# Decode tokens and the last inverse merge as whole 128 by 128 products, up weights in the main buffers, first results unpaused

## The chip, the cores and the metric

The kernel runs on one core of one Trainium2 chip. The metric is device time in microseconds. Three runs of the kernel before took 1026.06, 1026.82 and 1027.05 us; the median is 1026.82 us.

## What is computed

One decoder layer for 1024 prompt tokens and 64 decode tokens (8 sequences of 8 tokens). RMS-normalised input goes through one wide projection. A gated linear attention (GLA, 4 heads) and a gated DeltaNet (4 heads, keys and values 128 wide) run beside each other; each is gated, projected to 1024 channels, merged by sigmoid gates, projected again and added to the input; a per-layer embedding is added and a last RMSNorm follows. The part that the change is about most is the DeltaNet's chunk:

```python
    k_beta = k * beta[..., None]
    v_beta = v * beta[..., None]
    a_mat = jnp.where(strict, jnp.einsum('bhnid,bhnjd->bhnij', k_beta, k) * gamma, 0.0)
    t_mat = a_mat + jnp.eye(c, dtype=jnp.float32)
    solve = functools.partial(lax.linalg.triangular_solve, left_side=True, lower=True,
                              unit_diagonal=True)
    u = solve(t_mat, v_beta)
    w = solve(t_mat, k_beta * jnp.exp(decay)[..., None])
    qk = jnp.einsum('bhnid,bhnjd->bhnij', q, k) * gamma
    ...
    def step(s, inp):
        w_c, u_c, q_c, qk_c, k_c, d_c = inp
        v_new = u_c - jnp.einsum('bhcd,bhdv->bhcv', w_c, s)
        o_c = jnp.einsum('bhcd,bhdv->bhcv', q_c, s) + jnp.einsum('bhcs,bhsv->bhcv', qk_c, v_new)
        s = s * d_c[..., None, None] + jnp.einsum('bhcd,bhcv->bhdv', k_c, v_new)
        return s, o_c
```

The prompt starts from a zero state, the decode tokens from given states (`state_gla`, `state_gdn`, `state_conv`). All inputs and outputs are fp32.

## The kernel before

All activations lie with channels on the 128 partitions and tokens along the columns: 1024 prompt columns, then 64 decode columns. Every large product is made three times from split operands (`xh`, `xl` and `wh`, `wl`, type fp32r), in `prod`, one output tile of up to 416 columns after the other. These are called main products here. In the middle of the run they are those of the input projection (`ing`, `inza`, `inzb`, `ingsg`, `ingsh`), then come the up projections `py`, the output projection `ho` and the embedding `eg`, `ep`.

The branches are written as Python generators, run by `_Side`. After each six main products, `prod` calls `sd.tick()`, and each task goes one step on; `yield n` in a task lets n ticks pass. So TensorE's queue holds main products with a branch's small products strewn in between, in an order that is fixed when the program is built. Small products are plain fp32: the profiler shows two records for each (x2), and one for a transposing product.

The steps that the change touches:

- `conv_rest` (L781): short convolution of q, k or v of one head; the 64 decode columns go to `Ds`, a 128x64 tile. For q and k it makes token-row copies of the chunks (`ss`) and takes their squares; the decode columns get a product of their own (`ssS`, L840 for q, L842 for k).
- `gdn` (L852): decay matrix `Gm`, products `kq` (L898, L899; chunk 8 is that of the decode tokens), inverses of 32x32 blocks on VectorE (`B`), then merges to 64 (`z32`, `x32`) and to 128 (`z64` L974, `x64` L982, on 64x64 tiles of the array), then the chunk loop `ch` (L1006 to L1017), then rows out (`obT`, `obS` L1055).
- `gdn_sample` (L1062): the decode tokens against the given states: `sa` (L1081, then L1087 and L1091 on 64x64 tiles), and `dSb` (L1105), which updates the states in two products of 32 rows each.
- `gla` (L569): its decode part makes `attS` in two products of 64x64 (L718).
- `w_load`, `w_split`: a weight block is loaded to `wr`, then split by ScalarE (L173) and VectorE (L174). Most blocks go to `wh`, `wl` with three buffers each. The up weights go to `uh`, `ul`, in a pool `lp` that is opened when the pools of the branches are closed:

```python
    rec.close()
    lp = ctx.enter_context(tc.tile_pool(name="lp", bufs=1))
```

- `final` and `normed` (L1417, L1426): the last RMSNorm of column chunks 0 and 1 runs as a side task during the embedding of chunk 2; five ticks pass after each sum (`ssy`, L1422) and three before each store. Chunk 2 itself is done in two halves at the end of `embed` (L1463 to L1484).

Of the kernel before, what the change touches and what calls it, by code (L numbers as in the profile page):

```python
# [27 lines left out]
UW, HW = 1116, 512  # L28
# [3 lines left out]
C_ID, C_TRI, C_TRB, C_SEG, C_NEG, C_NGS, C_SCN, C_SEL, C_SL4 = 0, 128, 256, 384, 512, 640, 704, 768, 776  # L32
C_N = 780
# [70 lines left out]
def tile_hybrid_step(ctx: ExitStack, tc: tile.TileContext, xT, pT, wmain, wv0, wv1, wup, wout, wpg, wpl, wgate,  # L104
# [22 lines left out]
    def small(name):  # L127
        return kp.tile([P, P], F32, tag="sm", name=name, bufs=8)

    def col(name, w=NS):  # L130
        return kp.tile([P, NS], F32, tag="col", name=name, bufs=12)[:, 0:w]
# [19 lines left out]
    def bfree(n=1):  # L151
        sd.free_banks += n
# [199 lines left out]
    K = kp.tile([P, C_N], F32, tag="K", name="K")  # L352
    ident = K[:, C_ID:C_ID + P]
    tri = K[:, C_TRI:C_TRI + P]
    load(K, cst)

# [132 lines left out]
    def gdn_scalars():  # L489
# [32 lines left out]
        mm(ps[:, 32:36], K[:, C_TRB:C_TRB + P], gd[:, 8], start=True, stop=True)  # L522
        mm(ps[:, 64:96], ones, gd[:, 0:8], start=True, stop=True)
        mm(ps[:, 96:100], K[:, C_SEG:C_SEG + P], gd[:, 8], start=True, stop=True)
# [42 lines left out]
    def gla(hp):  # L567
# [131 lines left out]
        att_s, kem = small(f"attS{hp}"), small(f"kem{hp}")  # L699
        G.memset(att_s, 0.0)  # L700
        G.memset(kem, 0.0)
# [9 lines left out]
        for h2 in range(2):  # L711
            r = slice(64 * h2, 64 * h2 + 64)
            V.tensor_copy(kem[r, r], keS[r])
        yield from sd.banks(1)
        ps = rps(f"attS{hp}")
        for h2 in range(2):
            r = slice(64 * h2, 64 * h2 + 64)
            mm(ps[r, 0:NS], kS[r], qS[r], start=True, stop=True)  # L718
            V.copy_predicated(att_s[r, r], mks[r], ps[r, 0:NS])
        PE.transpose(ps[:, 128:256], kem, ident)  # L720
# [38 lines left out]
    cb, sss, sks, resv = {}, {}, {}, {}  # L759
# [21 lines left out]
    def conv_rest(kind, h, R, S):  # L781
# [12 lines left out]
        Ds = col(f"Ds{kind}{h}")  # L794
# [5 lines left out]
        if kind == 2:  # L800
# [15 lines left out]
            cb[kind, h] = (R, Ds)  # L816
# [6 lines left out]
        ss, r = sss[h], slice(64 * i, 64 * i + 64)  # L823
# [23 lines left out]
        cb[kind, h] = (D, Ds, R)  # L847

    def gdn(h):
# [20 lines left out]
        while (0, h) not in cb or (1, h) not in cb:  # L870
            yield 0
        q, q_s, _ = cb[0, h]
        k, k_s, kt = cb[1, h]
# [15 lines left out]

        for g in range(5):  # L890
            yield from sd.banks(1)
            ps = rps(f"kq{h}{g}")
            for c in range(2 * g, min(2 * g + 2, 9)):
                s = slice(c * P, (c + 1) * P) if c < 8 else slice(NP, T)
                m = P if c < 8 else NS
                o = (c % 2) * 256
                kc, qc = (k[:, s], q[:, s]) if c < 8 else (k_s, q_s)
                mm(ps[0:m, o:o + m], kc, kc, start=True, stop=True)  # L898
                mm(ps[0:m, o + P:o + P + m], kc, qc, start=True, stop=True)  # L899
                V.scalar_tensor_tensor(AT[0:m, s], ps[0:m, o:o + m], nbr2[0:m, c:c + 1], Gm[0:m, s],  # L900
                                       op0=ALU.mult, op1=ALU.mult)
                V.scalar_tensor_tensor(Gm[0:m, s], ps[0:m, o + P:o + P + m], rk[0:m, c:c + 1], Gm[0:m, s],
                                       op0=ALU.mult, op1=ALU.mult)
# [7 lines left out]
        for j in range(2):  # L911
            r = slice(32 * j, 32 * j + 32)
            load(scr_a[h][32 + j].rearrange("(s t) -> s t", s=32), AT[r, NP + 32 * j:NP + 32 * j + 32])
# [671 lines left out]
```

## Time and profile before

| | |
|---|---|
| median of three runs | 1026.82 us |
| the profiled execution | 1021.09 us |
| its span (first to last instruction) | 1019.3 us |
| granted TensorE clock, mean | 0.996 |
| TensorE busy | 1003.2 us, 7042 records |
| VectorE busy | 620.0 us, 1400 instructions |
| ScalarE busy | 397.1 us, 956 instructions |
| GpSimd busy | 36.6 us, 53 instructions |

The page's second part shows TensorE at 90% or more in 39 of 40 slices. A record's duration includes the fill of the array, and records overlap; what a product costs is the distance from its start to the start of the next one. A main product of 384 columns starts 0.17 us after the one before it while its record says 0.34 us.

### The profile page before, as it was taken

The page shows a single profiled execution, that of the slowest core. Times are in us where ns is not written, and L with a number is a line of the kernel's source. Part 1 is how long each engine was busy: PE and PEld are TensorE (multiplying, and loading weights), DVE is VectorE, ACT ScalarE, POOL GpSimd, SP SyncE. Part 2 cuts the span into 40 slices and gives each one's busy share as a digit, 9 for nine tenths or more (in the row PEclk, how much of TensorE's full clock was granted, in tenths as well). Part 3 has the DMA queues.
Part 4 walks back from the last instruction along what each step waited for, and adds up shares of the span by engine and source line. Part 5 has one row for each costly group of instructions (what it writes and reads, how often), then busy time and mean ns, then how long its engine had stood idle before and what let it go on. Part 6 is the DMA issues. An engine that isn't in the chain of part 4 may idle for free.

```text
span 1019.3 us, 17637 instructions
## 1 busy us (share of the span) xinstructions
PE 1003.2 (98%) x7042; PEld 962.0 (94%) x7042; DVE 620.0 (61%) x1400; ACT 397.1 (39%) x956; POOL 36.6 (4%) x53
## 2 busy tenths in 40 slices
PE   9999999999999999999999999999999999999996
PEld 7999999979999999999999999999999999999996
DVE  6785743455776679667866775554488323653347
ACT  6764634334314523452354224331233111533335
POOL 0000001011100001000000000000000000000000
PEclk9999999999999999999999999999999999999998
DMA  9011112222133021322132222003456332221015
GB/s 320 2 42 63 50 52 78 87 73 74 51 109 95 22 75 45 92 68 63 59 96 73 62 95 70 12 24 112 134 158 173 111 129 107 63 83 42 21 48 190
DMA packets 67027, 84.73 MB, mean 83 GB/s; under 512 B 26797, under 2 KB 51313, under 8 KB 66945
## 3 DMA queue, kind: packets, MB, share of 16 engines
q1 hardware_dynamic: 66672, 83.22, 26.1%
q8 instruction: 55, 0.90, 0.4%
q10 hardware_dynamic: 272, 0.39, 0.1%
q14 instruction: 28, 0.22, 0.1%
HBM read 65.38 MB, written 18.21 MB: 82 GB/s over the span
## 4 chain that ended last, share of the span: by engine, by line
PE 91%; DVE 5%; DMA 1%; ACT 1%; issue 1%; POOL 0%; SPq 0%; DVEq 0%; ACTq 0%
PE ing L288 12%; PE ingsg L288 9%; PE py L288 9%; PE ho L288 9%; PE ingsh L288 8%; PE eg L288 8%; PE inzb L288 5%; PE inza L288 5%; PE ep L288 2%; PE inka L288 2%; PE inqa L288 2%; PE v L402 2%; PE v L403 2%; PE v L405 1%; DVE B L927 1%; DVE tm L925 1%
## 5 line engine op out<-in xcount | busy, mean ns | idle before, releaser
L173 ACT CAST wh<-wr 128x1024 fp32r<-128x1024 f32 x59 | 61.8, 1049 | 164.3 <-PE ho L288 41.0
L174 DVE TENSOR_TENSOR wl<-wr,wh 128x1024 fp32r<-128x1024 f32 x59 | 72.0, 1222 | 72.0 <-ACT wh L173 71.1
L288 PE MATMUL ing<-xh,wh 128*128 128x384 f32 (+1 forms) x288 | 97.8, 340 | 0.0
L288 PE MATMUL ing<-xl,wh 128*128 128x384 f32 (+1 forms) x288 | 94.7, 329 | 0.0
L288 PE MATMUL ing<-xh,wl 128*128 128x384 f32 (+1 forms) x288 | 94.2, 327 | 0.0
L288 PE MATMUL ingsh<-xh,wh 128*128 128x384 f32 (+1 forms) x192 | 66.6, 347 | 0.0
L288 PE MATMUL ingsg<-xh,wh 128*128 128x384 f32 (+1 forms) x192 | 65.6, 342 | 0.0
L288 PE MATMUL eg<-Hh,wh 128*128 128x416 f32 (+1 forms) x192 | 63.6, 331 | 0.0
L288 PE MATMUL eg<-Hh,wl 128*128 128x416 f32 (+1 forms) x192 | 63.2, 329 | 0.0
L288 PE MATMUL ingsg<-xl,wh 128*128 128x384 f32 (+1 forms) x192 | 63.0, 328 | 0.0
L288 PE MATMUL ho<-Mh,wh 128*128 128x416 f32 (+1 forms) x192 | 63.0, 328 | 0.0
L288 PE MATMUL ingsh<-xl,wh 128*128 128x384 f32 (+1 forms) x192 | 62.9, 328 | 0.0
L288 PE MATMUL ingsg<-xh,wl 128*128 128x384 f32 (+1 forms) x192 | 62.9, 327 | 0.0
L288 PE MATMUL ingsh<-xh,wl 128*128 128x384 f32 (+1 forms) x192 | 62.9, 327 | 0.0
L288 PE MATMUL ho<-Ml,wh 128*128 128x416 f32 (+1 forms) x192 | 62.8, 327 | 0.0
L288 PE MATMUL ho<-Mh,wl 128*128 128x416 f32 (+1 forms) x192 | 62.8, 327 | 0.0
L288 PE MATMUL eg<-Hl,wh 128*128 128x416 f32 (+1 forms) x192 | 62.7, 327 | 0.0
L288 PEld LDWEIGHTS ing<-xh,wh 128*128 128x128 f32 x288 | 54.1, 188 | 2.2 <-issue 1.1
L288 PEld LDWEIGHTS ing<-xl,wh 128*128 128x128 f32 x288 | 54.2, 188 | 0.3 <-issue 0.2
L288 PEld LDWEIGHTS ing<-xh,wl 128*128 128x128 f32 x288 | 54.1, 188 | 0.2 <-issue 0.2
L789 DVE SCALAR_TENSOR_TENSOR D<-R,cw,D 128x1112 f32<-128x1112 f32 x36 | 49.2, 1368 | 2.6 <-ACT D L787 2.1
L1393 DVE SCALAR_TENSOR_TENSOR H<-ho,xres 128x416 f32<-128x416 f32 (+1 forms) x24 | 12.8, 535 | 57.7 <-PE ho L288 57.7
(432 smaller groups left out, 2764.1 us busy)
## 6 DMA issues: line engine op xcount, KB each, us to landing
wr<-in_wmain SPq DMA_DIRECT2D x38, 512.0 KB, 3.5
wr<-in_wpg SPq DMA_DIRECT2D x13, 512.0 KB, 3.5
xres<-in_xT SPq DMA_DIRECT2D x8, 544.0 KB, 4.5
wr<-in_wup SPq DMA_DIRECT2D x16, 256.0 KB, 2.7
wr<-in_wout SPq DMA_DIRECT2D x8, 512.0 KB, 3.6
gt<-gscrg SPq DMA_DIRECT2D x16, 208.0 KB, 2.3
gt<-gscrh SPq DMA_DIRECT2D x16, 208.0 KB, 2.4
out_yT<-y SPq DMA_DIRECT2D x8, 416.0 KB, 2.5
```

The costliest lines, as they stand in the source:

```text
L173: a = A.copy(wh, wr).ins
L174: b = (eng or V).tensor_tensor(wl, wr, wh.bitcast(F32), op=ALU.subtract).ins
L288: mm(ps[:, :w], l_, r_, start=i == 0, stop=i == len(seq) - 1)
L402: mm(ps[:, :n], h_, a_, start=k == 0, stop=False)
L403: mm(ps[:, :n], l_, a_, start=False, stop=False)
L405: mm(ps[:, :n], h_, b_, start=False, stop=k == 7)
L789: V.scalar_tensor_tensor(D[:, :n], R[:, i:n + i], cw[:, 4 * ci + i:4 * ci + i + 1], D[:, :n], op0=ALU.mult, op1=ALU.add)
L925: V.tensor_tensor(tv, Bv[:, j:j + 1, j + 1:32].broadcast_to([NBLK, j, n]), Bv[:, 0:j, j:j + 1].broadcast_to([NBLK, j, n]), op=ALU.mult)
L927: V.tensor_tensor(Bv[:, 0:j, j + 1:32], Bv[:, 0:j, j + 1:32], tv, op=ALU.add)
L1393: V.scalar_tensor_tensor(H[m][:, o:o + w], ps[:, :w], 0.5, xres[m][:, o:o + w], op0=ALU.mult, op1=ALU.add)
```

## The change

- The decode columns of q and k of one head share one 128x128 tile `kqs` (k in columns 0 to 63, q in 64 to 127); v has a tile `vs` with zeros behind it. One whole transposing product replaces L840 and L842, one whole product replaces chunk 8 of L898 and L899, and one transposing product replaces the two of L992.
- `Cs` (128x128, lower rows zero) holds the decode tokens' two 64x64 matrices side by side; L1087, L1091 and L1055 become whole 128x128 products.
- `z64` and `x64` run as whole products of 64 columns; GpSimd clears the rows of `X` and `Z` that would disturb them. `X` and `Z` get a ninth block (`HW` 576).
- The second pause of `gdn` before `z32` is 13 ticks and not 10.
- `dSb`'s first product is held behind the chunk loop's last product (`after`).
- `attS` is one whole product from a masked copy `km`.
- The up weights use `hw_main`.
- `final` waits one tick and not five, `normed` none and not three.
- The constants tile is split; `small` has 11 buffers, `col` 8.

```diff
-        yield from sd.banks(1)
-        ps = rps(f"ssS{h}{i}")
-        if kind == 0:
-            mm(ps[r, 0:P], Ds, ident, start=True, stop=True)
-        else:
-            PE.transpose(ps[r, 0:P], Ds, ident)
-        A.activation(ps[r, 0:P], ps[r, 0:P], AF.Square, accum_out=ss[r, 9 * i + 8:9 * i + 9])
-        bfree()
...
+        if (1 - kind, h) in cv:
+
+            yield from sd.banks(1)
+            ps = rps(f"ssS{h}")
+            PE.transpose(ps[:, 0:P], sm, ident)
...
+            if g == 4:
+                mm(ps[:, 0:P], kq_s, kq_s, start=True, stop=True)
...
-        yield 10
+        yield 13
...
+        G.memset(X[64:128, 0:8], 0.0)
+        G.memset(Z[0:64, 0:8], 0.0)
         for c in range(8):
-            mm(zv[64:128, c], ATv[0:64, c, 64:128], X[0:64, c], start=True, stop=True)
-        A.copy(Z[64:128], zv[64:128])
+            mm(zv[:, c], ATv[:, c], X[:, c], start=True, stop=True)
+        A.copy(Z[64:128, 0:8], zv[64:128])
...
         for c in range(8):
-            mm(zv[0:64, c], Z[64:128, c], ATv[64:128, c, 64:128], start=True, stop=True)
+            mm(zv[:, c], Z[:, c:c + 2].rearrange("p c n -> p (c n)"), ATv[:, c, 64:128], start=True, stop=True)
...
-            mm(ps[:, 0:P], Gm[:, s], vn, start=True, stop=True)
+            lastpe[h] = mm(ps[:, 0:P], Gm[:, s], vn, start=True, stop=True).ins
...
-        PE.transpose(ps[:, 0:NS], os_[hi], K[hi, C_ID + NS:C_ID + P])
-        A.mul(ob[h][:, NP:T], ps[:, 0:NS], nwh[:, 1:2])
+        PE.transpose(ps[:, 0:P], os_, ident)
+        A.mul(ob[h][:, NP:T], ps[:, NS:P], nwh[:, 1:2])
...
-        mm(ps[lo, 256:384], AT[lo, NP:T], vtS[lo], start=True, stop=True)
-        vn = small(f"vnS{h}")
-        A.mul(vn[lo], ps[lo, 256:384], brk[lo, 8:9])
+        mm(ps[:, 256:384], Cs, vtS, start=True, stop=True)
+        vn = vtS
+        A.mul(vn, ps[:, 256:384], brk[:, 8:9])
         yield 5
-        mm(ps[hi, 384:512], Gm[lo, NP:T], vn[lo], start=True, stop=True)
...
+        mm(ps[:, 384:512], Cs, vn, start=True, stop=True)
...
-            mm(pd[g], ktS[r], vb[r], start=True, stop=True)
+            e = mm(pd[g], ktS[r], vb[r], start=True, stop=True).ins
+            if g == 0 and h in lastpe:
+                after(e, lastpe[h])
...
-            wlist += [(wup[8 * br + m], 4, P, hw_up)]
+            wlist += [(wup[8 * br + m], 4, P, hw_main)]
...
-            yield 5
+            yield 1
         yield from normed(parts, pss, last)
 
-    def normed(parts, pss, last, waits=3, sizes=(2, 2, 2, 2)):
+    def normed(parts, pss, last, waits=0, sizes=(2, 2, 2, 2)):
```

TensorE's queue where the first head's states are updated. Before, as built:

```order
L288 MATMUL ing_2_4204<-xh_574,wl 128x320
L1105 MATMUL dSb_4256<-vbb_4166,ktS_3885 128x512
L1016 MATMUL ch_4211<-vn_4230,R_2518 128x128
L1017 MATMUL ch_4211<-vn_4230,Gm_2626 128x128
L1105 MATMUL dSb_4257<-vbb_4166,ktS_3885 128x512
L288 MATMUL ing_2_4204<-xh_574,wh 128x320
```

The same place in the changed kernel:

```order
L288 MATMUL ing_2_4215<-xh_580,wh 128x320
L1040 MATMUL ch_4222<-vn_4241,R_2527 128x128
L1041 MATMUL ch_4222<-vn_4241,Gm_2635 128x128
L1127 MATMUL dSb_4267<-vbb_4177,ktS_2866 128x512
L1127 MATMUL dSb_4268<-vbb_4177,ktS_2866 128x512
L288 MATMUL ing_2_4215<-xl_581,wh 128x320
```

The two `dSb` products stood apart, with two products of the chunk loop between them; now they stand side by side.

ScalarE's queue around the last two blocks of the z gate (`ztzb`), ahead of the up projection. Before:

```order
L1245 ACTIVATE ztzb_7300<-inzb_1_7275 128x384
L1245 ACTIVATE ztzb_7331<-inzb_2_7304 128x320
L1048 ACTIVATE ob_7311<-obT_7335,nwh 128x512
...
L1245 ACTIVATE ztzb_7406<-inzb_1_7381 128x384
L1245 ACTIVATE ztzb_7435<-inzb_2_7410 128x320
L173 CAST uh<-wr 128x512 x7
```

In the changed kernel:

```order
L1269 ACTIVATE ztzb_7308<-inzb_1_7270 128x384
L173 CAST wh<-wr 128x512
L1269 ACTIVATE ztzb_7337<-inzb_2_7312 128x320
...
L1269 ACTIVATE ztzb_7414<-inzb_1_7389 128x384
L173 CAST wh<-wr 128x512
L1269 ACTIVATE ztzb_7443<-inzb_2_7418 128x320
L173 CAST wh<-wr 128x512 x5
```

The first split of an up weight stood behind the last z block; now one stands a whole z block earlier and one more ahead of the last.

VectorE's queue at the end, from the embedding block before the last to the last chunk's squares (`y` are final results of chunk 1). Before:

```order
L1487 SCALAR_TENSOR_TENSOR et_10216<-et_10216,ep_10219 128x256
L1448 TENSOR_TENSOR y_10318<-H_8739,rsy_10138 128x416
L1488 SCALAR_TENSOR_TENSOR H_8739<-et_10216,H_8739 128x256
L1448 TENSOR_TENSOR y_10322<-H_8834,rsy_10138 128x416
L1448 TENSOR_TENSOR y_10322<-H_8925,rsy_10138 128x416
L1493 TENSOR_TENSOR acc_9248<-acc_9248,es_10217 128x256
L1448 TENSOR_TENSOR y_10326<-H_9016,rsy_10138 128x416
L1474 SCALAR_TENSOR_TENSOR et_10256<-et_10256,es_10257 128x128
L1446 SCALAR_TENSOR_TENSOR y_10326<-H_9107,pc,rsy_10138 128x416
L1477 TENSOR_TENSOR H_8834<-H_8834,et_10256 128x128
L1478 TENSOR_TENSOR es_10257<-H_8834 128x128
```

In the changed kernel:

```order
L1507 SCALAR_TENSOR_TENSOR et_10249<-et_10249,ep_10252 128x256
L1508 SCALAR_TENSOR_TENSOR H_8747<-et_10249,H_8747 128x256
L1513 TENSOR_TENSOR acc_9256<-acc_9256,es_10250 128x256
L1494 SCALAR_TENSOR_TENSOR et_10289<-et_10289,es_10290 128x128
L1497 TENSOR_TENSOR H_8842<-H_8842,et_10289 128x128
L1498 TENSOR_TENSOR es_10290<-H_8842 128x128
```

All `y` of chunks 0 and 1 now stand earlier, from the first embedding block of chunk 2 on.

## Rows read from the trace of the kernel before

**Rows 1.** The page's first part (engine, busy us and share of the span, instructions) and its fourth, the chain that ended last, by engine.

```profile
PE 1003.2 (98%) x7042; PEld 962.0 (94%) x7042; DVE 620.0 (61%) x1400; ACT 397.1 (39%) x956; POOL 36.6 (4%) x53
PE 91%; DVE 5%; DMA 1%; ACT 1%; issue 1%; POOL 0%; SPq 0%; DVEq 0%; ACTq 0%
```

**Rows 2.** Whom TensorE waited for, whole span: us in total, times, longest.

```profile
PE z L951 <- DVE X L943: 1.2, 1, 1.2
PE ssy L1471 <- DVE acc L1493: 1.1, 1, 1.1
PE o L562 <- DVE ssqa L553: 1.1, 1, 1.1
PE py L288 <- ACT uh L173: 1.0, 1, 1.0
```

**Rows 3.** Timeline of TensorE around `x64` of the first head (one main product left out): start us, duration us, what, rows x columns of the array's tile, partitions x columns that stream, count of records, and in brackets the idle time before.

```profile
335.35 0.34 PE L288 MATMUL ing<-xh,wl 128*128 128x384 f32 x1
335.62 1.14 PE L982 MATMUL x<-AT,Z 64*64 64x64 f32 x16
...
336.98 0.34 PE L288 MATMUL ing<-xl,wh 128*128 128x384 f32 x1
```

**Rows 4.** The same view where whole fp32 products with few columns follow each other (cumulated decays, `gds`).

```profile
124.07 0.30 PE L521 MATMUL gds<-gd,K 128*128 128x32 f32 x2
124.21 0.36 PE L522 MATMUL gds<-gd,K 128*128 128x4 f32 x2
124.43 0.39 PE L523 MATMUL gds<-gd,ones 128*128 128x32 f32 x2
```

**Rows 5.** The same view around a single whole fp32 product of 128 columns among main products (one main product left out).

```profile
377.40 0.33 PE L288 MATMUL ing<-xh,wh 128*128 128x384 f32 x1
377.57 0.38 PE L1012 MATMUL ch<-R,AT 128*128 128x128 f32 x2
...
377.97 0.34 PE L288 MATMUL ing<-xh,wl 128*128 128x384 f32 x1
```

**Rows 6.** The same view around `ssS`: of q (L840, a product on 64 columns of the array), and of k (L842, a transposing product); one main product is left out in each.

```profile
331.67 0.34 PE L288 MATMUL ing<-xh,wl 128*128 128x384 f32 x1
331.93 0.43 PE L840 MATMUL ssS<-K,Ds 128*64 128x128 f32 x2
...
332.58 0.33 PE L288 MATMUL ing<-xl,wh 128*128 128x384 f32 x1
...
346.25 0.34 PE L288 MATMUL inza<-xh,wl 128*128 128x384 f32 x1
346.42 0.27 PE L842 MATMUL ssS<-K,Ds 128*64 128x128 f32 x1
...
346.70 0.33 PE L288 MATMUL inza<-xl,wh 128*128 128x384 f32 x1
```

**Rows 7.** The same view around a 64x64 product of the decode tokens (`sa`, L1091), between a whole product and two main products, one of them left out.

```profile
384.80 0.39 PE L1007 MATMUL ch<-S,D 128*128 128x128 f32 x2
385.12 0.43 PE L1091 MATMUL sa<-vnS,Gm 64*64 64x128 f32 x2
...
385.76 0.34 PE L288 MATMUL ing<-xl,wh 128*128 128x384 f32 x1
```

**Rows 8.** The same view around the state updates `dSb`: of the first head (the two apart, two products of the chunk loop between them and a main product behind them left out), and of the last (side by side; the same three left out).

```profile
391.62 0.31 PE L288 MATMUL ing<-xh,wl 128*128 128x320 f32 x1
391.86 1.12 PE L1105 MATMUL dSb<-vbb,ktS 32*128 32x512 f32 x2
...
393.55 1.12 PE L1105 MATMUL dSb<-vbb,ktS 32*128 32x512 f32 x2
...
394.86 0.31 PE L288 MATMUL ing<-xl,wh 128*128 128x320 f32 x1
...
667.74 0.31 PE L288 MATMUL inzb<-xh,wl 128*128 128x320 f32 x1
...
668.42 1.13 PE L1105 MATMUL dSb<-vbb,ktS 32*128 32x512 f32 x4
...
669.76 0.34 PE L288 MATMUL inzb<-xl,wh 128*128 128x384 f32 x1
```

**Rows 9.** The same view around a decode row out, `obS` (one main product left out).

```profile
431.93 0.34 PE L288 MATMUL ing<-xh,wl 128*128 128x384 f32 x1
432.19 0.27 PE L1055 MATMUL obS<-K,os 64*128 64x64 f32 x1
...
432.65 0.31 PE L288 MATMUL ing<-xl,wh 128*128 128x320 f32 x1
```

**Rows 10.** Timeline of GpSimd, the one clearing of 512 columns in the first head's stretch.

```profile
330.48 0.53 POOL L1070 MEMSET kqm<- 128x512 f32 x1 [71.09 <-PE z L974]
```

**Rows 11.** Timelines of VectorE and of ScalarE at the end of the run.

```profile
1008.87 0.42 DVE L1493 TENSOR_TENSOR acc<-acc,es 128x256 f32<-128x256 f32 x1
1009.21 0.58 DVE L1448 TENSOR_TENSOR y<-H,rsy 128x416 f32<-128x416 f32 x1
1009.71 0.28 DVE L1474 SCALAR_TENSOR_TENSOR et<-et,es 128x128 f32<-128x128 f32 x1
1009.91 0.65 DVE L1446 SCALAR_TENSOR_TENSOR y<-H,pc,rsy 128x416 f32<-128x416 f32 x1
...
1009.42 1.28 ACT L1428 ACT_TABLE_LOAD   x1
```

More of the change, by code (lines that the diff above doesn't have):

```diff
@@ L351, in tile_hybrid_step @@
         load(wg[hp][0:16, :], wgate[:, hp * P:(hp + 1) * P])
-    K = kp.tile([P, C_N], F32, tag="K", name="K")
+    K = kp.tile([P, C_K], F32, tag="K", name="K")
     ident = K[:, C_ID:C_ID + P]
-    tri = K[:, C_TRI:C_TRI + P]
-    load(K, cst)
+    load(K, cst[:, 0:C_K])
+    tri, trb, seg = (small(n) for n in ("tri", "trb", "seg"))
+    for t, o in ((tri, C_TRI), (trb, C_TRB), (seg, C_SEG)):
+        load(t, cst[:, o:o + P])
     mk = kp.tile([P, P], U8, tag="mk", name="mk")
@@ L697, in gla @@
         load(gla_p[hp], Sprev[:, 1024 - P:1024])
-        att_s, kem = small(f"attS{hp}"), small(f"kem{hp}")
-        G.memset(att_s, 0.0)
-        G.memset(kem, 0.0)
+        att_s, kem, km = small(f"attS{hp}"), small(f"kem{hp}"), small(f"km{hp}")
+        for t in (att_s, kem, km):
+            G.memset(t, 0.0)
         S0 = [half(f"S0a{hp}{g}")[:, :512] for g in range(2)]
@@ L713, in gla @@
             V.tensor_copy(kem[r, r], keS[r])
+            V.tensor_copy(km[r, r], kS[r])
         yield from sd.banks(1)
         ps = rps(f"attS{hp}")
+        mm(ps[:, 0:NS], km, qS, start=True, stop=True)
+        PE.transpose(ps[:, 128:256], kem, ident)
         for h2 in range(2):
             r = slice(64 * h2, 64 * h2 + 64)
-            mm(ps[r, 0:NS], kS[r], qS[r], start=True, stop=True)
             V.copy_predicated(att_s[r, r], mks[r], ps[r, 0:NS])
-        PE.transpose(ps[:, 128:256], kem, ident)
         kmr = small(f"kmr{hp}")
@@ L793, in conv_rest @@
         yield 0
-        Ds = col(f"Ds{kind}{h}")
+        if kind == 2:
+            sm = small(f"vs{h}")
+            G.memset(sm[:, NS:], 0.0)
+            Ds = sm[:, 0:NS]
+        else:
+            if h not in kqs:
+                kqs[h] = small(f"kqs{h}")
+            sm = kqs[h]
+            Ds = sm[:, 0:NS] if kind == 1 else sm[:, NS:P]
         V.scalar_tensor_tensor(D[:, :NP], R[:, :NP], 1.0, D[:, :NP], op0=ALU.add, op1=ALU.mult)
@@ L822, in conv_rest @@
         i = 1 - kind
[L823 removed]
+        ss = sss[h]
         yield 4
@@ L869, in gdn @@
         yield 6
-        while (0, h) not in cb or (1, h) not in cb:
+        while ("s", h) not in cb or (0, h) not in cb or (1, h) not in cb:
             yield 0
-        q, q_s, _ = cb[0, h]
-        k, k_s, kt = cb[1, h]
+        q, _ = cb[0, h]
+        k, kt = cb[1, h]
+        kq_s, ktS = cb["s", h], kts[h]
         ss = sss[h]
@@ L888, in gdn @@
         yield 3
+        lo = slice(0, NS)
+        Cs = small(f"Cs{h}")
+        G.memset(Cs[NS:P], 0.0)
         for g in range(5):
@@ L1070, in gdn_sample @@
         G.memset(kq, 0.0)
[L1071 to L1075 removed]
+        for c in range(4):
+            V.tensor_copy(kq[:, c * P:(c + 1) * P].rearrange("p (b i) -> p b i", i=8)[:, 0:16:5],
+                          kq_s[:, 32 * c:32 * c + 32].rearrange("p (b i) -> p b i", i=8))
         yield 2
@@ L1295, in tile_hybrid_step @@
     lp = ctx.enter_context(tc.tile_pool(name="lp", bufs=1))
-    def hw_up(n, w):
-        return tuple(lp.tile([P, 512], F32R, tag=t, name=t, bufs=2).rearrange("p (k n) -> p k n", n=w)
-                     for t in ("uh", "ul"))
     for br in range(2):
```

87 lines of the change are left out of this document (44 added, 43 removed).

## Prediction

> **What bounds the kernel now.** I read first the page's busy times and its chain of waits by engine [rows 1]. TensorE is busy 98% of the span and holds 91% of the chain, so a part of the change is worth what it takes out of TensorE's queue, plus the few waits of that queue. The view of whom TensorE waited for came next [rows 2]: four waits of about 1 us each. Then I read the timeline of TensorE at each place the diff touches. A record's duration says little there, since records overlap; I use distances from one start to a later start and subtract the main products between. A main product of 384 columns is 0.173 us: 377.57 - 377.40 in [rows 5] shows 0.17, and longer runs give the third digit. By columns that makes 0.147 for one of 320.
>
> Three prices follow, all at the full granted clock (the 2.4 GHz level; the mean of the span is 0.996).
> - A whole fp32 product of 128 columns: 377.97 - 377.40 less two main products = 0.22 [rows 5]. With only 4 columns it is still 124.43 - 124.21 = 0.22 [rows 4], though with 32 columns the first of that run shows 124.21 - 124.07 = 0.14. I take 0.22 whatever the number of columns.
> - A transposing product: 346.70 - 346.25 less two main products = 0.10 [rows 6].
> - Leaving the whole array for a smaller tile: the main product ahead of `x64` is followed after 335.62 - 335.35 = 0.27 instead of 0.173 [rows 3], so about 0.1 going in; coming back costs about the same, as the whole sums below contain.
>
> **The change part by part: TensorE's queue.**
> - `z64`, `x64`. Eight small products between two main products take 336.98 - 335.35 - 2 x 0.173 = 1.28 us with both shape changes [rows 3]. As whole products they take 8 x 0.223 = 1.78. That is +0.50, two groups in four heads: **+4.0**. Bounds: the eight small ones cost (1.28 - 0.2)/8, about 0.13 with these edges and 0.117 inside the run; if whole products of 64 columns cost the 0.117 as well, a group takes 0.94 and the part is -2.8.
>
> The Trainium skill ("TensorEngine Tiling (Array Packing)", section "When to Use Tiling") favours tiles for contractions of up to 64 rows, because several products then run at once; it speaks against this edit. The trace agrees where two row groups are used, in [rows 8], but all eight of `x64` lie on one position of the array, and 1.28 us for them shows no overlap to lose. By that rule alone the part would be no cheaper than +4.0.
>
> - `sa`, L1087 and L1091. [Rows 7]: from L1007 to the second main product 385.76 - 384.80 = 0.96; less a whole product and a main product, 0.56 for one 64x64 product with its shape changes. Whole: 0.22. Eight of them at -0.34: **-2.7**.
> - `dSb`. Apart, in the first head: 394.86 - 391.62 less two main products of 320 = 2.95 for two `dSb` and two chunk products. Side by side, in the last head: 669.76 - 667.74 - 0.147 - 0.173 = 1.70 for the same four [rows 8]. The order shows the pair side by side now. Three heads stood apart: 3 x 1.25 = **-3.7**. The first product now waits behind the chunk loop's last one; what stands behind it in the queue is the second `dSb`, and the chunk products ahead are those that stood there anyway, so I count no idle time.
> - `ssS`. q's product goes: 332.58 - 331.67 - 2 x 0.173 = 0.56 [rows 6]; k's transposing one stays, on the whole array. Four heads: **-2.3**.
> - `obS`: 432.65 - 431.93 - 0.173 - 0.147 = 0.40 [rows 9] against 0.10 for a transposing product of the whole array: **-1.2**.
> - Chunk 8 of `kq`, two products on 64 columns, to one whole product; `trS`, one transposing product fewer; `attS`, two products of 64x64 to one whole. These I did not read one by one: two tiled products with their edges are about 0.4, one whole 0.22, so -0.2 x 4 = -0.8; -0.1 x 4 = -0.4; `attS` by the price of [rows 7], 0.56 plus one more product 0.12, less 0.22, = -0.46 in two branches, of which the first hides in the wait at `o` (L562) just behind it [rows 2]: -0.5 to -0.9, taken as -0.7. Together **-1.9**.
>
> The sum is 4.0 - 2.7 - 3.7 - 2.3 - 1.2 - 1.9 = **-7.8 us** of TensorE.
>
> **Waits.**
> - `z` (L951 behind VectorE's `X`): 1.2 us [rows 2], in the first head. Three more ticks put 18 main products, 18 x 0.173 = 3.1 us, ahead of it: **-1.2**, bounds 0 (if the other tasks' ticks were already all there was to give) and -1.2. Each head's later steps come 3.1 us later, which is covered while main products last.
> - `py` behind `uh`: 1.0 us [rows 2]. Its cause is order: the first split of an up weight stood behind the last z block on ScalarE, since its pool opens late. In the order of the changed kernel it stands a z block earlier: **-1.0**. What could be late next is the weight's load; SP's queue holds it far ahead.
> - The end. `ssy` waits 1.1 us for `acc`, which ends at 1009.29 behind final results `y` of chunk 1 [rows 2, 11]. Two `y` of 0.58 stand ahead of `acc` and two more, 0.58 and 0.65, ahead of L1474 and L1477 [rows 11]. In the new order none does. The first sum can start up to 1.1 earlier, and L1477 0.65 more; but ScalarE's table load of 1.28 from 1009.42 on [rows 11] also has to be done before `rsy`. Bounds -0.5 and -1.8; I take **-1.6**, since the order puts all of the `y` away.
> - What may come new: the burst of eight `y` (8 x 0.58 = 4.6 us on VectorE) now stands at the start of chunk 2, ahead of splits that the next embedding products need; with about 1 us of slack there I allow 0.3. `kem`, `km` and their copies need VectorE before the second branch's `attS`: 0.3. Together **+0.6**, bounds 0 and 2.
> - GpSimd's clearings of `X` and `Z` ahead of `z64`: 0.53 each, by the one clearing of 512 columns that [rows 10] shows, so 1.06; some 24 main products, 24 x 0.173 = 4.2 us, lie between `x32` and `z64` and hide them. Cost nothing; without that cover 1.06 x 4 = 4.2.
> - The other edits (constants split, buffers 11 and 8) move no instruction on TensorE; I count nothing, bounds +-0.5.
>
> Waits together: -1.2 - 1.0 - 1.6 + 0.6 = **-3.2**. All in all -7.8 - 3.2 = **-11.0**. The profiled execution, 1021.09 us (its span 1019.3), would be 1010.1. It stands 5.7 below the median of the runs, 1026.82; the same difference from that median gives **1015.8**.
>
> **Rivals.**
> - *Whole products are cheap when narrow.* If the streamed columns and not the weights set the price, `z64` and `x64` take 0.117 each and the part is -2.8, not +4.0: 1009.0. For it: 0.14 once in [rows 4]. Against it: 0.22 with 4 columns, directly behind it.
>
> The Trainium skill ("TensorE: Matmul & The Clock Gate", section "Back-to-back issue gap") gives one short price for all products of 1 to 64 columns, which is this rival. The same page's section "LDWEIGHTS (loading the stationary operand)" lets a weight load go by its columns, 128 here, and 0.22 with 4 columns [rows 4] agrees with that one.
>
> - *The waits only move.* TensorE's 7.8 us come out, but the pauses, the table load and the bursts of `y` end last where the old waits did: none of the 3.2, and about 0.5 more lost: 1026.8 - 7.8 + 0.5 = 1019.5. For it: waits of 1 us beside an engine that is 61% busy (VectorE) come and go with small shifts. Against it: two of the three have their cause in an order that is plainly gone.
> - *The other side: GpSimd holds up `z64`.* Its queue is in order, and the clearings can wait there behind another task's clearing or power that itself waits. TensorE then stops ahead of `z64` in every head, with all main products behind it. This decides from 11.0 / 4 = 2.75 us a head; with 4 us a head it is 1015.8 + 16 = 1031.8. For it: in [rows 10] the engine has one instruction after 71 us of idle time that `z` ended, so what it does hangs on others. Against it: 36.6 us of work in the whole span [rows 1], and 4.2 us of cover.
>
> **How the numbers follow.** The forecast 0.65, narrow products cheap 0.12, waits only move 0.18, GpSimd 0.05. The forecast's own range is 1013 to 1018.5: the waits' bounds (+1.1 and -0.2 at the end, +1.4 new, +1.2 `z`) and about 1.5 for the parts not read one by one. To hold 8 in 10 the range goes down to the first rival's 1009.0 and up past the second's 1019.5 to 1021.0. A measurement of this kernel tells 0.2%, 2 us, from no change. Faster: all of the first three cases but a few hundredths where a new wait eats more, 0.90; within 0.2%: 0.05; slower: 0.05.
>
> **What would show it.** In the profile of the changed kernel: TensorE busy about 8 us less; runs of eight whole products for `z64` and `x64` that take 1.78 us (0.94 would be the first rival); no 64x64 tile for `sa`; four `dSb` pairs, each of some 1.1 us; no `z32` and no `py` among the waits, and `ssy` with well under 1 us. A wait of `z64` behind GpSimd in several heads would make the prediction wrong, as would a new wait of over 2 us at the start of chunk 2 of the embedding.

## The result, and the profile after

The changed kernel takes 1015.28 us (median of five runs, 1013.61 to 1015.52). The kernel before took 1026.06 us beside it (five runs, 1022.96 to 1027.05). The ratio is 0.9895, 95% interval 0.9876 to 0.9913, so 8.9 to 12.7 us less. The forecast was 1015.8 us. The profiled execution of the changed kernel took 1013.61 us, its span is 1011.8 us and its mean granted clock 0.998. Against the profiled execution of before, 1021.09 us, that is only 7.5 us less. Why the two differences disagree is the main question of what follows. The notation of the rows is that of the rows read before; PE is TensorE, PEld its weight loads, DVE VectorE, ACT ScalarE, POOL GpSimd.

The busy times of the changed kernel, from the first part of its page, answer to [rows 1]:

```profile
PE 996.1 (98%) x7018; PEld 965.8 (95%) x7018; DVE 620.3 (61%) x1408; ACT 397.0 (39%) x956; POOL 42.1 (4%) x75
```

TensorE is busy 7.1 us less. Its waits over the whole span answer to [rows 2] (us in total, times, longest):

```profile
PE o L564 <- DVE ssqa L555: 1.8, 1, 1.8
PE kq L915 <- DVE Gm L918: 1.5, 1, 1.5
...
PE ssy L1499 <- DVE es L1498: 1.3, 2, 1.0
PE ch L1036 <- ACT qs L1034: 0.7, 3, 0.2
...
PE attS L719 <- DVE km L716: 0.3, 1, 0.3
```

The row of `ssy` behind `es` has its counterpart in the kernel before:

```profile
PE ssy L1479 <- DVE es L1478: 1.5, 2, 1.2
```

The waits of `z32`, of `py` and of `ssy` for `acc` are gone, as forecast; `ssy` still waits for `es`. Two large ones are new: `kq` behind `Gm`, and `ch` behind ScalarE's `qs`. The 0.3 us that were allowed for `km` came (`attS`). The burst of `y`, allowed another 0.3, costs nothing: TensorE's timeline shows no wait of over 0.06 us between 600 and 1000 us. The wait at `o` is 0.7 us longer, because `attS` ahead of it is shorter: there nothing is won, as forecast.

Here is the timeline of TensorE around `x64` of the first head in the changed kernel (start, duration, line, tile of the array, count of records), the place of [rows 3]:

```profile
337.34 0.30 PE L288 MATMUL ing<-xh,wl 128*128 128x320 f32 x1
337.48 1.89 PE L1007 MATMUL x<-AT,Z 128*128 128x64 f32 x16
339.19 0.39 PE L288 MATMUL ing<-xh,wh 128*128 128x320 f32 x1
339.42 0.31 PE L288 MATMUL ing<-xl,wh 128*128 128x320 f32 x1
```

From the main product ahead to the second one behind, less two main products of 0.147: 339.42 - 337.34 - 0.294 = 1.79 us. The forecast was 8 x 0.223 = 1.78. Eight products that stream 64 columns through the whole array cost as much as eight of 128 columns.

The same view where the first head's states are updated, the place of [rows 8]:

```profile
391.01 0.31 PE L288 MATMUL ing<-xh,wh 128*128 128x320 f32 x1
391.16 0.38 PE L1040 MATMUL ch<-vn,R 128*128 128x128 f32 x2
391.38 0.39 PE L1041 MATMUL ch<-vn,Gm 128*128 128x128 f32 x2
391.69 1.13 PE L1127 MATMUL dSb<-vbb,ktS 32*128 32x512 f32 x4
392.75 0.41 PE L288 MATMUL ing<-xl,wh 128*128 128x320 f32 x1
```

Both `dSb` products stand side by side on two row groups, and 1.06 us pass to the next main product, where the two took 1.05 us each before. And `sa`, the place of [rows 7]:

```profile
375.37 0.39 PE L1031 MATMUL ch<-S,D 128*128 128x128 f32 x2
375.60 0.39 PE L1109 MATMUL sa<-vs,Cs 128*128 128x128 f32 x2
375.74 0.42 PE L288 MATMUL ing<-xh,wh 128*128 128x384 f32 x1
376.00 0.34 PE L288 MATMUL ing<-xl,wh 128*128 128x384 f32 x1
```

376.00 - 375.37 = 0.63 us from the whole product ahead to the second main product behind; before it was 0.96 [rows 7].

### The profile page after: what moved, and what is told of

The parts are those of the page before. It is cut to its first block, busy times and chain, and to the rows that moved or that the text cites. A ratio compares the mean times of both kernels' runs of the same rounds, so it can differ in the third digit from the quotient of the medians.

```text
span 1011.8 us, 17649 instructions
## 1 busy us (share of the span) xinstructions
PE 996.1 (98%) x7018; PEld 965.8 (95%) x7018; DVE 620.3 (61%) x1408; ACT 397.0 (39%) x956; POOL 42.1 (4%) x75
## 4 chain that ended last, share of the span: by engine, by line
PE 71%; DVE 3%; ACT 1%; POOL 0%; issue 0%; DVEq 0%; ACTq 0%; POOLq 0%
PE ing L288 12%; PE eg L288 9%; PE py L288 9%; PE ho L288 9%; PE ingsg L288 6%; PE ingsh L288 5%; PE inzb L288 5%; PE inza L288 3%; PE ep L288 2%; PE ch L1036 1%; PE ch L1040 1%; PE ch L1041 1%; PE x L1007 1%; PE z L999 1%; PE kq L915 1%; DVE D L792 1%
## 5 line engine op out<-in xcount | busy, mean ns | idle before, releaser
L173 ACT CAST wh<-wr 128x1024 fp32r<-128x1024 f32 (+1 forms) x75 | 71.6, 958 | 212.3 <-PE py L288 43.0
L174 DVE TENSOR_TENSOR wl<-wr,wh 128x1024 fp32r<-128x1024 f32 (+1 forms) x75 | 83.0, 1107 | 83.9 <-ACT wh L173 82.5
```

Source lines behind the costliest of these rows:

```text
L173: a = A.copy(wh, wr).ins
L174: b = (eng or V).tensor_tensor(wl, wr, wh.bitcast(F32), op=ALU.subtract).ins
```

## The new waits in the trace

**`kq` behind `Gm`.** GpSimd raises k's sums of squares to a power (`rk`). The three rows below are that instruction in the kernel before, in the changed kernel, and in an experiment told of further down (`e_knorm`), each from the timeline of GpSimd:

```profile
256.57 2.71 POOL L877 TENSOR_TENSOR rk<-tk,mh 128x9 f32<-128x9 f32 x1 [1.69 <-DVE tk L876]
```

```profile
269.08 1.82 POOL L893 TENSOR_TENSOR rk<-tk,mh 128x9 f32<-128x9 f32 x1 [11.94 <-DVE tk L892]
```

```profile
258.82 1.81 POOL L904 TENSOR_TENSOR rk<-tk,mh 128x9 f32<-128x9 f32 x1 [0.48 <-DVE tk L903]
```

In the first head k is convolved before q. Before, k's decode columns had a product and a square of their own, so the ninth sum of k was there at 256 us. Now one product serves k and q, it comes when q is ready too, and `rk` starts 12.5 us later. What hangs on it, from the changed kernel's timeline of VectorE and TensorE:

```profile
270.93 0.17 DVE L896 TENSOR_TENSOR sk<-tk,rk 128x9 f32<-128x9 f32 x1 [1.23 <-POOL R L771]
...
271.77 1.22 DVE L903 TENSOR_TENSOR R<-R,kes 128x1024 f32<-128x1024 f32 x1
272.90 0.35 DVE L918 SCALAR_TENSOR_TENSOR Gm<-kq,rk,Gm 128x128 f32<-128x128 f32 x1
...
273.30 0.49 PE L915 MATMUL kq<-D 128*128 128x128 f32 x2 [1.51 <-DVE Gm L918]
```

The row of `sk` names a clearing of `R` as its releaser; that stands right behind `rk` on GpSimd, and `rk` ends at 270.90. The product at 273.30 needs a free bank, which `Gm` releases at the end of this chain, and TensorE stops for 1.51 us. In the other heads k comes last, and `kq` waits 0.09 us at most.

**`ch` behind `qs`.** Before, the chunk loop found its operands ready behind `sa`. There `ch` followed 0.17 us behind the main product ahead [rows 5]. Now TensorE gets there 0.3 us earlier, but ScalarE's queue does not. The same place in the changed kernel, ScalarE and TensorE:

```profile
376.78 0.36 ACT L1034 ACTIVATE qs<-ch,ed 128x128 f32<-128x128 f32 x1
...
377.19 0.49 PE L1036 MATMUL ch<-R,AT 128*128 128x128 f32 x2
```

`ch` starts 0.05 us after `qs` ends, and 0.33 us behind the main product ahead (376.86). The same happens behind `dSb` (0.23 us of idle time at 395.64). For the second head I followed the same 175 main products, from the one behind `x64` to the one behind `dSb` and the next chunk step: 46.79 us before, 45.31 after, 1.48 less. By the parts (`sa` 2 x 0.33, `dSb` 1.25, chunk 8 of `kq` 0.17) it would be 2.08. So 0.6 us came back in such waits, and as much in the third head; some 0.7 in the first and little in the fourth. This is the first profile of the changed kernel. In six of the ten profiles of it and its variants another wait stands in the first head, `ch` behind VectorE's `S`, of 0.15 us (the second profile, `a_again`) to 0.81 us (`e_upool`); none of the four profiles of the kernel before and its variants has it.

## The experiments

All were timed beside the kernel before, on three chips. The medians of before in the three groups were 1024.59, 1023.37 and 1023.07 us. `e_` kernels are edits of the changed kernel, `b_` kernels of the one before. The changed kernel itself was timed in the first group and in the runs of the result, so the other groups are compared with it across chips. Before's executions at a clock of 0.996 or more have medians of 1021.9, 1022.2 and 1021.2 us on the three: differences of about 1 us between chips tell nothing.

**Both kernels again (`b_again`, `a_again`).** No edit.

> The kernel before, unchanged, against itself. In the two profiles shown so far the change took 7.5 us off (1021.09 to 1013.61), in the medians of the runs 10.8 (1026.06 to 1015.28). If the profiled execution of before was only a quick one, its runs here spread from about 1021 to 1027 with a granted clock that goes with the time, and the ratio is 1.000 within 0.002. If the run with a profile is quicker by itself, only the profiled one is near 1021 and all others near 1026.

> The changed kernel, unchanged, on the same chip as the runs of before. If the sum of the prediction is right as a difference of medians: 10 to 12 us below before (ratio 0.988 to 0.990). If the difference of the two profiles is the right one: 7 to 8 us below (0.992 to 0.993).

The kernel before against itself: ratio 1.0002 (0.9986 to 1.0019), 12 runs from 1021.52 to 1026.92 us. The changed kernel: 1015.91 us (1015.33 to 1016.42), ratio 0.9907 (0.9890 to 0.9925), 7.7 to 11.3 us less: between the two expectations. The granted clock of each execution sorts the times of before. Of the 64 executions in the three groups, 18 have a mean clock of 0.996 or more (median 1021.87 us), 19 have 0.994 or 0.995 (1023.34), and 27 have 0.993 or less (1026.13). Of the changed kernel's ten, six have 0.996 or more (1015.39) and four 0.994 or 0.995 (1015.71); none is lower. So the profiled execution of before, with a clock of 1.00 from 210 to 230 and from 315 to 335 us, was a quick one. The three runs that the prediction took for the reference (1026.06 to 1027.05 us) belong by their times to the lowest group, and with the change that group is gone.

Where the clock falls is seen by stretches. The changed kernel from 210 to 230 us, in its first profile and in the second (the stretch and its length, busy us and instructions of PE, PEld, DVE, ACT and POOL, then the granted clock as a share of 2.4 GHz, the DMA engines' share and GB/s):

```profile
210.00:230.00 20.00, 17.62 (x214) 14.56 (x213) 10.21 (x24) 8.67 (x42) 4.28 (x6) 1.00 0.28 85
```

```profile
210.00:230.00 20.00, 17.76 (x198) 14.08 (x197) 9.54 (x22) 6.79 (x33) 3.26 (x5) 0.83 0.28 80
```

In this stretch lies the wait at `o` of the first GLA pair (1.8 us). In one execution the clock stays at 1.00, in another the mean is 0.83, and the main product behind comes 2.4 us later against the products ahead, the ones from the second on 2.6 us. Both kernels have this wait (1.1 us before), and of the 14 profiles of all kernels seven show the fall here, two of four of the kernel before and its variants, five of ten of the changed one and its variants. So it explains the spread of each and not the difference. The second place follows below.

**`z64` and `x64` on 64x64 tiles again (`e_tiles`).**

```diff
-        G.memset(Z[:, 8], 0.0)
...
-        G.memset(X[64:128, 0:8], 0.0)
-        G.memset(Z[0:64, 0:8], 0.0)
...
-            mm(zv[:, c], ATv[:, c], X[:, c], start=True, stop=True)
+            mm(zv[64:128, c], ATv[0:64, c, 64:128], X[0:64, c], start=True, stop=True)
...
-            mm(zv[:, c], Z[:, c:c + 2].rearrange("p c n -> p (c n)"), ATv[:, c, 64:128], start=True, stop=True)
+            mm(zv[0:64, c], Z[64:128, c], ATv[64:128, c, 64:128], start=True, stop=True)
```

> The changed kernel with z64 and x64 back on 64x64 tiles, and without GpSimd's clearings for them. By the price of the rows (0.22 for a whole product of 64 columns, whatever it streams) each of the eight groups gets 0.5 to 0.56 us shorter: 4 to 4.5 us less than the changed kernel, about 1011. By the rival (a whole product with 64 columns costs 0.117) it gets 2.8 us longer, about 1018. If what is saved is taken back by waits in the chunk loop behind, as part of sa's saving seems to be, it is between 1 and 3 us less.

1010.55 us (1010.35 to 1013.32), ratio 0.9861 (0.9840 to 0.9882), 5.4 us under the changed kernel of the same group (four runs and five). The timeline of TensorE at `x64`:

```profile
339.79 0.30 PE L288 MATMUL ing<-xh,wl 128*128 128x320 f32 x1
340.02 1.14 PE L1004 MATMUL x<-AT,Z 64*64 64x64 f32 x16
341.10 0.42 PE L288 MATMUL ing<-xh,wh 128*128 128x320 f32 x1
```

341.10 - 339.79 = 1.31 us, where the changed kernel has 339.19 - 337.34 = 1.85. Against the second profile of the changed kernel each of the eight groups is 0.51 to 0.54 us shorter, 4.2 in all, of which the chunk loops give 0.6 back. The price is as forecast, the rival of cheap narrow products is out, and this part of the change costs time. The traces account for 4.2 - 0.6 = 3.6 of the 5.4 us; the rest they do not show, and executions of one kernel differ by as much.

**k's decode columns of the first head squared at once (`e_knorm`).**

```diff
+        alone = kind == 1 and (0, h) not in cv
+        if alone:
+            yield from sd.banks(1)
+            ps = rps(f"ssK{h}")
+            PE.transpose(ps[0:NS, 0:P], sm[:, 0:NS], ident)
+            kts[h] = small(f"ktS{h}")
+            V.tensor_copy(kts[h][0:NS], ps[0:NS, 0:P])
+            A.activation(ps[0:NS, 0:P], ps[0:NS, 0:P], AF.Square, accum_out=ss[0:NS, 8:9])
+            bfree()
...
-            for r, o in ((slice(0, NS), 8), (slice(NS, P), 17)):
+            for r, o in ((slice(0, NS), 8), (slice(NS, P), 17))[first:]:
...
```

In the loop `first` is true where k's part is done already.

> The changed kernel, but where k is done before q (the first head alone) k's decode columns get their own transposing product and square at once. One transposing product more, +0.1 us on TensorE. Theory: the 1.5 us wait of kq (L915) behind Gm in the changed kernel is there because k's norm, with GpSimd's power of 1.8 us in it, now waits for q's squares; then the wait goes and the kernel is 1.2 to 1.6 us shorter, about 1013.8. Rival: the wait comes from TensorE being early there; then it stays at 1.3 to 1.6 us and the time is the same within 0.3 us.

1015.87 us (1012.78 to 1016.37), ratio 0.9901 (0.9881 to 0.9921): no difference in the median. The trace has no wait at `kq` any more, and `rk` starts at 258.82, as shown above. So the dependency is the cause. But VectorE's `tk` now stands ahead of what `oS` needs, and TensorE waits there:

```profile
258.81 0.30 PE L564 MATMUL oS<-K,orowaS 128*128 128x128 f32 x1 [0.50 <-DVE tk L903]
```

Behind `kq` its trace is 0.7 us ahead of the changed kernel's, less than half of the 1.5, at a distance that the times can't tell.

**Ten ticks ahead of `z32` (`e_pause10`).**

```diff
-        yield 13
+        yield 10
```

> The changed kernel with a pause of 10 ticks ahead of z32, as before. By the profile's wait alone (1.2 to 1.6 us at z32 in the first head): 1.2 to 1.6 us more than the changed kernel, 1016.5 to 1017. Second theory: in the slower half of before's runs the mean granted clock is 0.991 and the time 1025.5 to 1027, against 0.997 and about 1021.5 in the quicker ones; the changed kernel never went under 0.994. If TensorE's stop ahead of z32 is where the clock falls in those runs, runs of 0.991 come back here and the median is 3 to 4 us above the changed kernel, 1018.5 to 1020. If not, the lowest clock stays at 0.994.

1017.87 us (1015.26 to 1019.99), ratio 0.9937 (0.9917 to 0.9958). The lowest clock is 0.994. The trace shows why this is not the same wait as in before (VectorE, then TensorE):

```profile
319.82 0.44 DVE L965 STREAM_TRANSPOSE X<-AT 32x256 f32<-32x256 f32 x1
320.32 0.69 PE L973 MATMUL z<-X,AT 32*32 32x32 f32 x30 [0.39 <-DVE X L965]
```

The group is split in two by the order that was built, nine main products stand between its parts, and the stop is 0.39 us, not 1.2. With the second visit to small tiles it costs about 1.0 us in the trace of the first head. The profiled execution is one of the two quick ones (1015.27 us); the other four took 1017.8 to 1020.0 us at 0.994 or 0.995, and no trace shows what they lost. The test of the clock was thereby not made here.

**A pool of their own for the up weights (`e_upool`).**

```diff
+    def hw_up(n, w):
+        return tuple(lp.tile([P, 512], F32R, tag=t, name=t, bufs=2).rearrange("p (k n) -> p k n", n=w)
+                     for t in ("uh", "ul"))
...
-            wlist += [(wup[8 * br + m], 4, P, hw_main)]
+            wlist += [(wup[8 * br + m], 4, P, hw_up)]
```

> The changed kernel with the up weights in a pool of their own again, opened after the branches. By the profile's wait: py behind the first split comes back with 1.0 us, 1.0 more than the changed kernel, about 1016.7. If this stop and not z32's is where the clock falls in the slower runs of before, runs of 0.991 come back here and the median is 3 to 4 us above the changed kernel.

1016.69 us (1014.05 to 1018.53), ratio 0.9926 (0.9907 to 0.9944), 0.8 to 1.4 us more than the changed kernel. The wait is back with 1.0 us and the next product comes 1.19 us later against the changed kernel's. None of its six executions is under 0.994: nothing here speaks for this stop as the place.

**`sa` on 64x64 tiles (`e_satiles`).**

```diff
-        mm(ps[:, 256:384], Cs, vtS, start=True, stop=True)
+        mm(ps[lo, 256:384], Cs[lo, 0:64], vtS[lo], start=True, stop=True)
...
-        mm(ps[:, 384:512], Cs, vn, start=True, stop=True)
+        mm(ps[hi, 384:512], Cs[lo, 64:128], vn[lo], start=True, stop=True)
...
```

> The changed kernel with sa's second and third product on 64x64 tiles again, now from Cs. By the sum each of the eight costs 0.31 to 0.34 us more on TensorE: 2.5 to 2.7 us more in all. If the chunk loop takes part of that back (in the changed kernel ch waits 0.15 to 0.25 us for ScalarE behind sa, where before it waited for nothing), the steps behind sa lose those waits and it is only 1 to 1.8 us more.

1017.74 us (1015.43 to 1019.65), ratio 0.9937 (0.9918 to 0.9956), 1.8 to 2.5 us more than the changed kernel (1015.91 and 1015.28). The timeline shows both halves:

```profile
379.04 0.39 PE L1031 MATMUL ch<-S,D 128*128 128x128 f32 x2
379.36 0.43 PE L1109 MATMUL sa<-vs,Cs 64*64 64x128 f32 x2
379.72 0.45 PE L288 MATMUL ing<-xh,wh 128*128 128x384 f32 x1
380.00 0.34 PE L288 MATMUL ing<-xl,wh 128*128 128x384 f32 x1
...
381.06 0.38 PE L1036 MATMUL ch<-R,AT 128*128 128x128 f32 x2
```

380.00 - 379.04 = 0.96 us again, 0.33 more; but `ch` at 381.06 follows the main product ahead (380.88) after 0.18 us, with no wait. In three heads the first of the two `sa` products loses 0.31 and gets 0.26 back at `ch`. That is 3 x 0.36 + 0.62 = 1.7 us, as the second theory said.

**`dSb` not held (`e_noafter`).**

```diff
-            if g == 0 and h in lastpe:
-                after(e, lastpe[h])
```

> The changed kernel without the dependency that holds dSb's first product. In the built order the two dSb products then stand apart in all four heads, with two products of the chunk loop between them. By the rows 1.25 us each: 5.0 us more than the changed kernel, about 1020.7. If the stretch behind takes it back (S0's addition and the next step are not waited for), still 5.0; if the chunk loop's waits behind dSb shrink, 3.5 to 4.5.

1020.17 us (1017.81 to 1021.57), ratio 0.9961 (0.9943 to 0.9978), some 4.3 to 4.9 us more. In the trace each head loses 1.34 us at this place, and three of them gain some 0.38 in the chunk loop behind: 4 x 1.34 - 3 x 0.38 = 4.2. The first head's two products, apart again:

```profile
393.13 1.12 PE L1127 MATMUL dSb<-vbb,ktS 32*128 32x512 f32 x2
394.18 0.49 PE L1040 MATMUL ch<-vn,R 128*128 128x128 f32 x2
394.50 0.39 PE L1041 MATMUL ch<-vn,Gm 128*128 128x128 f32 x2
394.82 1.12 PE L1127 MATMUL dSb<-vbb,ktS 32*128 32x512 f32 x2
```

**The pauses of the final results again (`e_final`).**

```diff
-            yield 1
+            yield 5
         yield from normed(parts, pss, last)
-    def normed(parts, pss, last, waits=0, sizes=(2, 2, 2, 2)):
+    def normed(parts, pss, last, waits=3, sizes=(2, 2, 2, 2)):
```

> The changed kernel with final's and normed's pauses of five and three ticks again. By the prediction's end term: the final results of chunk 1 stand ahead of the last sum of squares again, ssy waits about 1.1 us for acc, and the kernel is 1.6 us longer (0.5 to 1.8), about 1017.5. If the chain from the last eg products over the table load sets the end by itself, it is the same within 0.3 us.

1015.64 us (1014.39 to 1015.80), ratio 0.9921 (0.9899 to 0.9943): in time no difference from the changed kernel. In the trace the wait is back:

```profile
1002.68 0.71 PE L1491 MATMUL ssy<-acc,ones 128*128 128x128 f32 x4 [1.14 <-DVE acc L1513]
```

and from the last main products to the end it is 1.6 us longer than in the changed kernel's profile, while the first products were up to 0.9 us quicker in this execution. All six executions had a clock of 0.996 or 0.997. So the term is shown in the trace, and not confirmed by the times.

**Thirteen ticks alone, and the main buffers alone, in the kernel before (`b_pause13`, `b_wmain`).**

```diff
-        yield 10
+        yield 13
```

```diff
-            wlist += [(wup[8 * br + m], 4, P, hw_up)]
+            wlist += [(wup[8 * br + m], 4, P, hw_main)]
```

> The kernel before with 13 ticks ahead of z32 and nothing else. By the profile's wait: 1.2 us less than before. Of the executions of before about half show a granted clock of 0.991 to 0.993 and 1025.4 to 1027 us; neither the pause nor the up weights' pool alone brought such runs into the changed kernel. If z32's wait makes them in before, none of six runs is under 0.994 here and the median is 2.5 to 3.5 us below before's; if it has no part in them, about half of the runs are still there and the median is 1 to 1.5 us below.

> The kernel before with the up weights in the main buffers and nothing else. By the profile's wait: py's 1.0 us goes, 1.0 us less than before. If py's wait makes the runs of 0.991 to 0.993, none of six is under 0.994 and the median is 2.5 to 3.5 us below before's; if it has no part in them, about half of the runs are still there and the median is 0.8 to 1.2 us below.

`b_pause13`: 1021.24 us, 12 runs, ratio 0.9976 (0.9961 to 0.9990), 1.0 to 4.0 us less, with a median 1.8 below before's, between its two cases; two of its 12 executions have a clock of 0.993 or less. In its trace the main products behind `z32` come 1.7 us earlier against those ahead, the wait of 1.2 us and 0.4 to 0.5 around it. `b_wmain`: 1024.08 us, 12 runs, ratio 1.0005 (0.9989 to 1.0020); six of 12 are that low. In its trace `py` comes without its wait, 1.19 us earlier against the products ahead (1.3 from its second product on), but its times don't show that. The profile of `b_wmain` has a mean clock of 0.992, and its timeline of TensorE shows what happens in the first head:

```profile
320.69 1.00 PE L951 MATMUL z<-X,AT 32*32 32x32 f32 x30 [1.47 <-DVE X L943]
321.62 0.69 PE L288 MATMUL ing<-xl,wh 128*128 128x384 f32 x1
322.11 0.52 PE L288 MATMUL ing<-xh,wl 128*128 128x384 f32 x1
322.43 0.52 PE L288 MATMUL ing<-xh,wh 128*128 128x384 f32 x1
322.75 0.52 PE L288 MATMUL ing<-xl,wh 128*128 128x384 f32 x1
...
324.30 0.34 PE L288 MATMUL ing<-xh,wh 128*128 128x384 f32 x1
324.47 0.33 PE L288 MATMUL ing<-xl,wh 128*128 128x384 f32 x1
```

After a stop of 1.47 us at `z32` the main products start 0.32 us apart instead of 0.17: the lower level of 1.2 GHz, until about 324.2. The same stretch by windows, in `b_wmain`, in the first profile of the kernel before, where TensorE stops for 1.2 us, and in `b_pause13`, where it doesn't stop there:

```profile
315.00:335.00 20.00, 18.53 (x184) 17.33 (x183) 11.33 (x15) 8.73 (x23) 0.53 (x1) 0.91 0.46 116
```

```profile
315.00:335.00 20.00, 18.78 (x192) 17.19 (x191) 13.10 (x21) 11.91 (x33) 0.53 (x1) 1.00 0.44 115
```

```profile
315.00:335.00 20.00, 20.00 (x203) 18.77 (x201) 14.90 (x25) 12.18 (x33) 0.00 (x0) 1.00 0.43 117
```

So the stop at `z32` costs its own 1.2 to 1.6 us, and in one of the three profiles that have it the clock falls behind it as well. Against the first profile of before, the main products of `b_wmain` come 1.8 us later ahead of `z32` and 3.5 behind it; the stop is 0.25 us longer there, so about 1.4 us go to the fall. With this stop, in before and `b_wmain`, 33 of 76 executions have 0.993 or less. In the changed kernel and its eight variants, where the stop is absent or 0.39 us long, it is 1 of 56. So the change as a whole takes the lowest group away. That the stop at `z32` alone makes this group is not shown: on the chip of `b_pause13` before has 6 of 23 such executions and `b_pause13` 2 of 12, which the numbers can't tell apart. Nor does the length of a stop decide it: `b_again` stops for 1.57 us at `z32` with no fall behind it, and the changed kernel's stop of 1.5 us at `kq` is followed by none in any of the eight profiles that have it. What makes the two low executions of `b_pause13` stays open, since no trace caught one.

**The two helpful edits together (`e_best`).** The edits of `e_tiles` and `e_knorm`.

> The changed kernel with both edits that helped alone: z64 and x64 on 64x64 tiles, and k's decode columns of the first head squared at once. Without it the medians were 1015.9 (changed kernel), 1010.6 (tiles alone) and 1015.9 (k alone, whose trace is 0.7 us ahead behind kq). If the parts add, 1009.8 to 1010.2, ratio to before 0.985 to 0.986; if k's wait is only replaced by another (oS behind it, 0.5 us), the same as the tiles alone within 0.3.

1010.27 us (1007.74 to 1011.95), ratio 0.9867 (0.9843 to 0.9890). It is faster than both kernels, by some 5 us than the changed one. Its trace is 5.8 us ahead of the changed kernel's first profile: 4.2 at `z64` and `x64`, about 0.7 at `oS` and `kq`, and 1.2 in the first products, which vary from execution to execution; the chunk loops give a little back. That it beats the tiles alone is not shown.

## Why the prediction came out

The time was met, 1015.28 against 1015.8. The sum behind it was not: it said 11.0 us less at the same clock, and the two profiles, both at the upper level but for about their last 7 and 4 us, show 7.5.

- **Prices of products: right.** `z64` and `x64` +0.54 x 8 = +4.3 (forecast +4.0). `sa` -0.33 x 8 = -2.6 (-2.7). `dSb`: the first head takes 1.70 us for the four products, as the last one did before, so -3.7 (-3.7). `obS` about -1.1 (-1.2), `ssS` about -1.9 (-2.3), `kq`, `trS`, `attS` together -1.8 (-1.9). The sum is -6.8 for -7.8; TensorE's busy time says -7.1. That a main product of 320 columns takes 0.147 us is right by distances; "by columns" 0.173 would give 0.144.
- **Waits gone: right, and priced a little low.** The idle times are `z32` -1.2, `py` -1.0, and the end -1.6 in the traces (-1.2, -1.0, -1.6). By the distances of main products, which hold what a stop costs beside its idle time, they are worth -1.7 (`b_pause13`), -1.3 (`b_wmain`, `e_upool`) and -1.7; for `z32` that is beyond the bound of 1.2.
- **New waits: the step that failed.** "Together +0.6, bounds 0 and 2" measured about +3.5: 1.5 at `kq` and some 2 in the chunk loops; the 0.3 at `km` comes on top. With the idle times the terms give -6.8 - 3.8 + 3.8 = -6.8, with the distances -6.8 - 4.7 + 3.8 = -7.7, for the 7.5 of the two profiles. Two sentences are behind it. For `ssS` I priced the product that goes and not what its result feeds: k's norm now waits for q. For `dSb` "I count no idle time", and for `sa` nothing at all, though TensorE gets ahead of a chain on VectorE and ScalarE that has not become shorter. `e_knorm` and `e_satiles` show the one and the other. Taking the wait at `kq` away gives back 0.7 us of its 1.5 only, since another wait stands behind it.
- **The clock: not in the sum.** The lower executions of before lose some 4 us against the quick ones (1026.13 against 1021.87). The two falls that traces show cost 2.6 us at `o` (`a_again`) and about 1.4 at `z32` (`b_wmain`), together 4.0; that such an execution of before has both is an estimate from these two numbers, as no trace of one exists. The change removes the stop at `z32`, and executions of 0.993 or less are all but gone. I took a difference read at the upper level from a median, 1026.82, of runs whose times lie with the lowest group. This made up for the missing 3.5 us. So the forecast was met by luck, through two errors that cancel: at 0.996 or more the medians are 1021.87 and 1015.39, 6.5 us apart, and in the first group of experiments the two medians are 8.7 apart (1024.59 and 1015.91), where the sum said 11.0 and the runs of the result 10.8.
- **The rivals.** Cheap narrow products: out by `e_tiles`. Waits only move: three of the old ones went, and new ones of about 3.5 us came; at one and the same clock this is nearly what happened (6.5 to 7.5 us less, where it said 7.3). GpSimd holding up `z64`: no such wait is in the list of waits.

The Trainium skill ("TensorEngine Tiling (Array Packing)", section "Key Properties") says that a change of tiling mode drains TensorE. The rows agree that such a change has a price: 0.32 us from a whole product to a 64x64 one in `e_satiles`, 0.23 between two whole ones at the same place in the changed kernel. Paid once in a run of eight and each time by a single one, this price makes single small tiles dear and a run of eight cheap.

## What to carry to other kernels

A small product on part of the array is worth making whole when it stands alone among whole ones, since it pays for the change of tile going in and coming out (0.33 us more for `sa`); a run of eight on one tile is not, since each whole product costs 0.22 us however few columns it streams, and one of such a run about 0.16 with the change of tile shared out (0.54 us less for the eight of `x64`). When two products are merged, look up what each result feeds, because the earlier consumer now waits for the later operand. And a microsecond saved on the bounding engine between two steps of a chain counts only as far as the chain's other engines were ahead.

## What was not expected of the hardware

A stop of TensorE of 1.5 us was followed by main products 0.32 us apart for about 2.5 us in one execution of `b_wmain`, and in the first profile of before a stop of 1.2 us at the same place was followed by none of this (clock 1.00 from 315 to 335 us, next products 0.17 apart), nor was the stop of 1.57 us in `b_again`. The 64 executions of one and the same program lie between 1020.36 and 1027.66 us; the 18 of them at 0.996 or more still spread from 1020.36 to 1023.29, so the clock is not the whole of it.
